# Weight passes in another order, and more seven-product pairs in the down projection, some with their weight sums made by DMA

## The chip, the cores and the metric

The kernel runs on one core of one Trainium2 chip. The metric is device time in microseconds of one execution; lower is better. Before the change the median of three runs is 1387.19 us (1386.93 to 1387.28).

## The reference

One layer of a hybrid decoder on 256 tokens of width 2048, all in float32:

```
h  = RMSNorm(x);  z = h @ W_in               # all projections of both kinds of heads, and two gates
A  = forgetting attention (8 heads of 128);  M = mLSTM (4 heads, 128 / 256)
merged = sigmoid(g_A) * (A @ P_A) + sigmoid(g_M) * (M @ P_M)
x  = x + merged @ W_out
u  = causal_dwconv3(RMSNorm(x) @ W_up)       # 2048 x 11264, each channel over three tokens
x  = x + (silu(u_gate) * u_val) @ W_down     # 5632 x 2048
```

The part at issue is the last two lines, the up product and the last product (the down projection), and in one detail the mLSTM's q and k projections.

## The kernel before, in words

**Products in parts.** TensorE multiplies float32 here in a one-pass form of rounded numbers. To keep accuracy each operand is split in a high and a low part: weights into `wh` (ScalarE, L170) and `wl = w - wh` (VectorE, L171), activations likewise (L198, L199). A product is then three passes: high by high, high by low, low by high.

**Weights.** They come in chunks of 1 MB ([128, 2048] float32), loaded on SP's queue into three buffers `raw` (L132). `split_sub` makes pieces of 1024 (or 512) columns of them, in four buffers each for `wh` and `wl`. `next_sub` hands a piece to TensorE, asks for the loads of the next two chunks, and has one to three further pieces split ahead. So a load waits until the third chunk before it has been split to its end.

**The up product** (`block_a`, `products_a`) has the weights as the stationary operand and 256 tokens as the moving one. For each 128 rows of the contraction there is a pass of 512 columns (`wh` by both parts of the activation, side by side) and one of 256 (`wl` by the high part). A block is 16 such pairs, 5632 rows of the output in 88 blocks by two halves `up` each; the convolution, gate and split of the result (`up_evac` and what follows) run on ScalarE and VectorE beside it. The mLSTM's q and k (`mq`, `mk`, 8 blocks) use the same function. `j` counts the 44 pairs of blocks (a gate and a value block); two `j` give a pair `m` of activation tiles, 22 pairs in all.

**The last product** (`s_block`, names `y0` and `y1` for the two halves of the output's columns) goes over these 22 pairs; here the activations are stationary and 512 weight columns move. A pair is a 2 by 2 block matrix (two tiles of tokens, two of the contraction, two of output columns). A plain pair ("p" in `Y_PAIRS`) takes eight products, 24 passes. A pair "S" uses Strassen's scheme in Winograd's form: seven products, 21 passes. For it sums of activations are made during up (`put_sums`, VectorE) and kept in DRAM (`s_dram`, written and read on POOL's queue; tiles `se` with a single buffer and `s_ops`), and sums of weights are made by VectorE just before their split: `b` (L155, 1024 columns), `b21` (L162, 512) and `t13` (L165, 512). A pair S has four pieces: the weights b11 and b22 as they are, b21, and the sums twice. Products of the four sub-blocks gather in PSUM (`y0q`, and `y0p` for those added to several results); after the last S some additions (`late`) bring them together.

**Order.** Every engine runs its instructions in order; a scheduler at build time sets the order on each engine from the program and its dependencies, and semaphores connect them. POOL's queue, in up, holds one write of `se` for each S, and in the last product the loads of `s_ops` and of the residual `xr`.

Of the kernel before, what the change touches and what calls it, by code (L numbers as in the profile page):

```python
# [10 lines left out]
F32 = mybir.dt.float32  # L11
# [6 lines left out]
P = 128  # L18
# [14 lines left out]

PLAIN = "p" * 8
G_PAIRS = "pSpSpSpp"
WO_PAIRS = "pSpSpSpp"
Y_PAIRS = "pp" + "SSp" * 2 + "Sp" + "SSp" * 3 + "Spp"
N_S = Y_PAIRS.count("S")  # L40

# [19 lines left out]
def trunk(ctx: ExitStack, tc: tile.TileContext, a):  # L61
# [28 lines left out]

    chunks, subs_of = [], []

    def add_chunk(ap, n, pieces=("whole", "whole")):

        subs_of.extend((len(chunks), i, kind) for i, kind in enumerate(pieces))
        chunks.append((ap, n, ap.tensor.name))

    def add_b(ap, n):
# [4 lines left out]
        add_chunk(a["w_mog0"][i], 2 * (MOG[0] + MOG[1]))  # L103
    add_b(a["w_mog1"], MOG[2])

    def add_pairs(ap, patterns):
        for i, kind in enumerate("".join(patterns)):
            pieces = ("b", "b21", "t13", "t24") if kind == "S" else ("whole", "whole")
            add_chunk(ap[i], 2048, pieces)

    for name in ("w_fox", "w_mqk", "w_mv"):
        add_b(a[name], 512)
# [21 lines left out]
    def split_sub(j):  # L134
        if j >= len(subs_of) or j in subs:
            return
        i, s, kind = subs_of[j]
# [3 lines left out]
        n = 512 if kind == "b21" else chunks[i][1] // 2  # L141
        raw, sums = raws[i], s_tiles.get("sums")


        if kind == "whole":
            src = raw[:, s * n : (s + 1) * n]
        elif kind == "b":
            src = raw[:, 512:1536]
            if s_tiles["of"] != chunks[i][2]:
                s_tiles["of"] = chunks[i][2]  # L150
                s_tiles["sums"] = a8(f"sums{i}", [2048])
            sums = s_tiles["sums"]

            with tc.issue_after(last_of["wl"].ins):
                nc.vector.tensor_tensor(  # L155
                    sums[:, :1024].rearrange("p (i c) -> p i c", i=2),
                    raw[:, :512].unsqueeze(1).to_broadcast([P, 2, 512]),
                    src.rearrange("p (i c) -> p i c", i=2), ALU.subtract,
                )
        elif kind == "b21":  # L160
            src = raw[:, 1536:]
            nc.vector.tensor_tensor(sums[:, 1024:1536], raw[:, 1024:1536], sums[:, :512], ALU.subtract)  # L162
        elif kind == "t13":
            src = sums[:, :1024]
            nc.vector.tensor_tensor(sums[:, 1536:], raw[:, 1536:], sums[:, 1024:1536], ALU.subtract)  # L165
# [4 lines left out]
        nc.scalar.activation(wh[:, :n], src, AF.Copy)  # L170
        last_of["wl"] = nc.vector.tensor_tensor(  # L171
            wl[:, :n], src, wh[:, :n].bitcast(F32), ALU.subtract
        )
        subs[j] = (wh[:, :n], wl[:, :n])
# [42 lines left out]
    def put_sums(src, dst, keep):  # L217

        a11, a21, a12, a22 = (src[:, i * P : (i + 1) * P] for i in range(4))
        n = 4 if keep else 3
        sv = scratch("sv", [P, n * P])
        s2, s3, s4 = (sv[:, i * P : (i + 1) * P] for i in range(3))
        s1 = sv[:, 3 * P :] if keep else a21
        nc.vector.tensor_tensor(s3, a21, a11, ALU.subtract)
        nc.vector.tensor_tensor(s1, a21, a22, ALU.add)
        nc.vector.tensor_tensor(s2, s1, a11, ALU.subtract)
        nc.vector.tensor_tensor(s4, a12, s2, ALU.subtract)
        put(dst[0], dst[1], sv)  # L230

    def mm(out, lhsT, rhs, start, stop):
# [47 lines left out]
    def s_block(name, pairs, s_ops, pattern, pools, dst, add=True, per_piece=0):  # L280


        q = [[pools[0](f"{name}q{tok}{h}") for h in range(2)] for tok in range(2)]
        ps, late, left = {}, [], pattern.count("S")
        n_s = left

        def prod(out, x, w, c, first, last):
            wh, wl = w[0][:, c * 512 : (c + 1) * 512], w[1][:, c * 512 : (c + 1) * 512]
            mm(out, x[1], wh, first, False)
            mm(out, x[0], wh, False, False)  # L290
            mm(out, x[0], wl, False, last)

        def piece():
            w = next_sub(4)
            for _ in range(min(2, len(late))):
                late.pop(0)()
            run_tasks(per_piece)
            return w

        def tt(o, x, y):  # L300
            late.append(lambda: nc.vector.tensor_tensor(o, x, y, ALU.add))

        for m, kind in enumerate(pattern):
            def op(i, tok):
                t = slice(tok * P, (tok + 1) * P)
                return pairs[m][:, i, 0, t], pairs[m][:, i, 1, t]

            if kind == "p":
                last = m == len(pattern) - 1
                ws = [piece(), piece()] if last else []  # L310

                todo = (
                    [(i, tok, h) for h in range(2) for tok in range(2) for i in range(2)] if last
                    else [(i, tok, h) for i in range(2) for h in range(2) for tok in range(2)]
                )
# [24 lines left out]
            if add:  # L340
                u3 = scratch("u3", [P, 512])
                late.append(lambda: nc.scalar.activation(u2, ps[1], AF.Copy))
                tt(c11, c11, ps[1])
                tt(u2, u2, ps[6])
                tt(u3, u2, ps[7])
                tt(u2, u2, ps[5])
                tt(c21, c21, u3)
                tt(u3, u3, ps[5])
                tt(c12, c12, u2)
                tt(c22, c22, u3)  # L350
            else:
                late.append(lambda: nc.scalar.activation(c11, ps[1], AF.Copy))
                tt(u2, c11, ps[6])
                tt(c21, u2, ps[7])
                tt(c12, u2, ps[5])
                tt(c22, c21, ps[5])
        for f in late:
            f()
        return q
# [36 lines left out]
    upper = const.tile([P, P], F32, name="upper")  # L396
    ones = const.tile([P, P], F32, name="ones")
    mhalf = const.tile([P, 8], F32, name="mhalf")
    mask_qk = const.tile([P, P], BF16, name="mask_qk")
    mask_st = const.tile([P, P], BF16, name="mask_st")  # L400

# [4 lines left out]

    def when_there(x):

        return nc.gpsimd.tensor_copy(mhalf[:, :1], x[:, :1].bitcast(F32))

    def make_constants():
        nc.gpsimd.memset(mhalf, -0.5)
# [517 lines left out]
    for j in range(NF):  # L930
# [19 lines left out]
        put_pair(g_pairs[m], gv)  # L950


    s_pos = [m for m, kind in enumerate(Y_PAIRS) if kind == "S"]
    ring = []

    def load_sums():
# [103 lines left out]
```

## Time and profile before

| | |
|---|---|
| median of three runs | 1387.19 us |
| the profiled execution, its own time | 1377.91 us |
| its span | 1376.1 us |
| granted TensorE clock | 1.000 |
| up product, about 667 to 1144 us | TensorE busy 477.0, VectorE 397.2, ScalarE 283.2 of 477.0 us |
| last product y0, 1144 to 1258 us | TensorE 113.7, VectorE 108.5, ScalarE 65.7 of 113.7 us |
| last product y1, 1258 to 1372 us | TensorE 113.7, VectorE 105.8, ScalarE 61.2 of 113.8 us |
| DMA over the span | 284 MB, mean 206 GB/s |

How to read it: a row of the page's groups names line, engine, operation, output and inputs, and the count. PE is TensorE's matmul, PEld its weight load. The chain that ended last is followed back from the last instruction; its pieces in order of time tell how long a run of passes of one kind took, with their count (`x48`). A window's row lists start and end, length, the busy time of each engine with its count of instructions, the granted clock, the DMA share and GB/s.

### The profile page before, as it was taken

To read this page: it belongs to the slowest core of one execution; us is meant where nothing else is said; L and a number is where in the kernel's file an instruction comes from. 1 tells how busy PE (TensorE), PEld (TensorE's weight loads), DVE (VectorE), ACT (ScalarE), POOL (GpSimd) and SP (SyncE) were. 2 spreads that over 40 slices of the span, in tenths; PEclk is the share of its full clock that TensorE was granted. 3 is DMA by queue.
4 is the path that set the end of the run, shared out by engine and by line. 5 is a ranking of instruction groups with operands and counts; after the bars stand their busy time and mean duration, and the time that the engine had idled before them with its cause. 6 is when DMAs were issued, how large, how long until landed. Compare 5 with 4: busy or idle time off the path is not lost.

```text
span 1376.1 us, 18451 instructions
## 1 busy us (share of the span) xinstructions
PE 1369.0 (99%) x6922; PEld 1158.1 (84%) x6922; DVE 1096.9 (80%) x1569; ACT 775.3 (56%) x1112; POOL 43.2 (3%) x77
## 2 busy tenths in 40 slices
PE   9999999999999999999999999999999999999998
PEld 8978888888888888888888888888888888878776
DVE  5655766556888867899888887888888888998998
ACT  6655554445665544465756565555555555564553
POOL 2101000000000000000000000000000000000000
PEclk9999999999999999999999999999999999999999
DMA  9644554443555556465555555555555566778853
GB/s 323 237 179 167 181 206 153 169 155 133 188 212 186 214 210 232 178 228 201 209 196 209 196 206 191 208 206 195 196 202 208 206 226 237 245 256 302 292 201 119
DMA packets 44649, 284.12 MB, mean 206 GB/s; under 512 B 5072, under 2 KB 5088, under 8 KB 13840
## 3 DMA queue, kind: packets, MB, share of 16 engines
q1 hardware_dynamic: 39168, 260.20, 52.6%
q0 software_dynamic: 5248, 22.74, 4.9%
q8 instruction: 54, 0.88, 0.3%
q14 instruction: 35, 0.29, 0.1%
q10 hardware_dynamic: 144, 0.02, 0.0%
HBM read 274.02 MB, written 8.91 MB: 206 GB/s over the span
## 4 chain that ended last, share of the span: by engine, by line
PE 99%; DVE 0%; DMA 0%; ACT 0%; issue 0%; ACTq 0%
PE up L233 35%; PE p L233 6%; PE y1q L233 6%; PE y0q L233 6%; PE mog L233 3%; PE fq L233 3%; PE g0q L233 3%; PE mv L233 3%; PE fk L233 3%; PE fv L233 3%; PE y0p L233 3%; PE y1p L233 3%; PE wo0q L233 2%; PE g1q L233 2%; PE g3q L233 2%; PE g2q L233 2%
## 5 line engine op out<-in xcount | busy, mean ns | idle before, releaser
L170 ACT ACTIVATE wh<-raw 128x1024 fp32r<-128x1024 f32 (+2 forms) x496 | 494.0, 1011 | 403.2 <-PE up L233 108.5
L171 DVE TENSOR_TENSOR wl<-raw,wh 128x1024 fp32r<-128x1024 f32 (+2 forms) x496 | 573.2, 1164 | 184.4 <-ACT wh L170 179.0
L233 PE MATMUL up<-h,wh 128*128 128x512 f32 x1408 | 488.8, 394 | 0.0
L233 PE MATMUL up<-h,wl 128*128 128x256 f32 x1408 | 390.2, 277 | 0.0
L233 PEld LDWEIGHTS up<-h,wh 128*128 128x128 f32 x1408 | 264.0, 188 | 61.4 <-DVE h L202 0.3
L233 PEld LDWEIGHTS up<-h,wl 128*128 128x128 f32 x1408 | 264.3, 188 | 0.2
L170 ACT ACTIVATE wh<-sums 128x1024 fp32r<-128x1024 f32 x78 | 82.8, 1062 | 118.4 <-PE y1q L233 24.6
L171 DVE TENSOR_TENSOR wl<-sums,wh 128x1024 fp32r<-128x1024 f32 x78 | 95.4, 1224 | 30.8 <-ACT wh L170 30.0
L918 DVE SCALAR_TENSOR_TENSOR t<-u,cst,t 128x256 f32<-128x256 f32 x176 | 84.9, 482 | 3.7 <-ACT t L916 0.7
L233 PE MATMUL p<-wh,am 128*128 128x512 f32 x256 | 79.6, 392 | 0.0
L233 PE MATMUL y1q<-wh,ghl 128*128 128x512 f32 x208 | 64.2, 390 | 0.0
L233 PE MATMUL y0q<-wh,ghl 128*128 128x512 f32 x208 | 64.2, 390 | 0.0
L233 PEld LDWEIGHTS p<-wh,am 128*128 128x128 f32 x256 | 47.6, 188 | 9.7
L916 ACT ACTIVATE t<-u,cst 128x256 f32<-128x256 f32 x88 | 52.0, 591 | 2.6 <-DVE u L913 2.2
L233 PE MATMUL p<-wl,am 128*128 128x512 f32 x128 | 49.9, 390 | 0.0
L155 DVE TENSOR_TENSOR sums<-raw 128x1024 f32<-128x1024 f32 x39 | 47.6, 1219 | 0.0
L233 PEld LDWEIGHTS y1q<-wh,ghl 128*128 128x128 f32 x208 | 39.1, 188 | 8.1
L233 PEld LDWEIGHTS y0q<-wh,ghl 128*128 128x128 f32 x208 | 39.0, 188 | 8.0
L233 PE MATMUL mog<-wh,hT 128*128 128x348 f32 (+1 forms) x192 | 42.5, 332 | 0.8 <-ACT wh L170 0.8
L233 PE MATMUL g0q<-wh,hN 128*128 128x512 f32 x128 | 41.2, 402 | 0.0
L233 PE MATMUL y1q<-wl,ghl 128*128 128x512 f32 x104 | 40.5, 390 | 0.0
L233 PE MATMUL y0q<-wl,ghl 128*128 128x512 f32 x104 | 40.5, 390 | 0.0
(370 smaller groups left out, 2110.0 us busy)
## 6 DMA issues: line engine op xcount, KB each, us to landing
raw<-in_w_up SPq DMA_DIRECT2D x88, 1024.0 KB, 4.8
raw<-in_w_dn SPq DMA_DIRECT2D x44, 1024.0 KB, 5.2
raw<-in_w_g SPq DMA_DIRECT2D x32, 1024.0 KB, 4.8
raw<-in_w_fox SPq DMA_DIRECT2D x24, 1024.0 KB, 4.9
raw<-in_w_p SPq DMA_DIRECT2D x16, 1024.0 KB, 4.9
raw<-in_w_out SPq DMA_DIRECT2D x16, 1024.0 KB, 4.9
s_ops<-s_dram POOLq DMA_DIRECT2D x12, 768.0 KB, 4.5
raw<-in_w_mqk SPq DMA_DIRECT2D x8, 1024.0 KB, 4.8
```

The lines of the kernel that those rows point to most:

```text
L155: nc.vector.tensor_tensor(sums[:, :1024].rearrange("p (i c) -> p i c", i=2), raw[:, :512].unsqueeze(1).to_broadcast([P, 2, 512]), src.rear ...
L170: nc.scalar.activation(wh[:, :n], src, AF.Copy)
L171: last_of["wl"] = nc.vector.tensor_tensor(wl[:, :n], src, wh[:, :n].bitcast(F32), ALU.subtract)
L233: last_of["mm"] = nc.tensor.matmul(out, lhsT, rhs, start=start, stop=stop)
L916: nc.scalar.activation(t, u[:, 2:], AF.Identity, scale=w[2], bias=w[3])
L918: nc.vector.scalar_tensor_tensor(out=t, in0=u[:, i : i + S], scalar=w[i], in1=t, op0=ALU.mult, op1=ALU.add)
```

## The change

1. `products_a` issues its passes in twos: two of 512 columns for two neighbouring contraction tiles, then the two of 256.
2. `Y_PAIRS` goes from `ppSSpSSpSpSSpSSpSSpSpp` to `pSZpSZSpSZpSZSpSZpSZpp`: 14 of 22 pairs with seven products instead of 12; eight are S, six are of a new kind Z.
3. For a Z the four blocks of weight sums lie ready in a DRAM tile `t`. They are made during the up product by six transfers on POOL's queue (three copies and three that add to what is there), one step for each `j`, each step behind a small copy that waits for `gv` of that `j`. Both halves have six, so there are 12 tiles and 72 transfers. In the last product a Z loads 1536 columns of its weights and 2048 of its `t`; its pieces need no sums on VectorE.
4. The signs of the sums are turned so that weights are only added (a DMA can add); activation sums and the last additions turn theirs to match. The waiting copy writes to a tile of its own, `seen`.

```diff
-Y_PAIRS = "pp" + "SSp" * 2 + "Sp" + "SSp" * 3 + "Spp"
-N_S = Y_PAIRS.count("S")
+Y_PAIRS = "p" + "SZpSZSp" * 2 + "SZpSZpp"
+N_S = len(Y_PAIRS) - Y_PAIRS.count("p")
...
     def add_pairs(ap, patterns):
         for i, kind in enumerate("".join(patterns)):
-            pieces = ("b", "b21", "t13", "t24") if kind == "S" else ("whole", "whole")
-            add_chunk(ap[i], 2048, pieces)
+            if kind == "Z":
+                t = dram.tile([P, 2048], F32, name=f"t{len(z_sums)}")
+                z_sums.append((t, ap[i]))
+                add_chunk(ap[i][:, 512:], 1536, (1024, 1536))
+                add_chunk(t, 2048)
+            else:
+                add_chunk(ap[i], 2048, ("b", "b21", "t13", "t24") if kind == "S" else None)
+
+    def sums_in_dram(i):
+
+        t, w = z_sums[i]
+        q = lambda x, n: x[:, n * 512 : (n + 1) * 512]
+        b12, b11, b22, b21 = (q(w, n) for n in range(4))
+        put_to = lambda o, x: lambda: nc.gpsimd.dma_start(o, x)
+        add_to = lambda o, x: lambda: nc.gpsimd.dma_start(o, x, accum_op=ALU.add)
+        return [
+            put_to(
+                t[:, :1024].rearrange("p (i c) -> p i c", i=2),
+                b12.unsqueeze(1).to_broadcast([P, 2, 512]),
+            ),
+            add_to(t[:, :1024], w[:, 512:1536]),
+            put_to(q(t, 2), q(t, 0)), add_to(q(t, 2), b22),
+            put_to(q(t, 3), q(t, 2)), add_to(q(t, 3), b21),
+        ]
...
     def products_a(z, act, ks, wh, wl, first, last):
 
-        for q, k in enumerate(ks):
-            ws = slice(q * P, (q + 1) * P)
-            mm(z, wh[:, ws], act[k].rearrange("p l s -> p (l s)"), first and q == 0, False)
-            mm(z[:, :S], wl[:, ws], act[k][:, 0, :], False, last and q == len(ks) - 1)
+
+        for q in range(0, len(ks), 2):
+            two = [(slice(i * P, (i + 1) * P), act[ks[i]]) for i in (q, q + 1)]
+            for i, (ws, x) in enumerate(two):
+                mm(z, wh[:, ws], x.rearrange("p l s -> p (l s)"), first and q + i == 0, False)
+            for i, (ws, x) in enumerate(two):
+                mm(z[:, :S], wl[:, ws], x[:, 0, :], False, last and q + i == len(ks) - 1)
...
         nc.vector.tensor_tensor(gv[:, (j % 2) * S : (j % 2 + 1) * S], sg, t, ALU.mult)
+
+        now = [(i, j - 1 - 3 * i) for i in range(len(z_sums)) if 0 <= j - 1 - 3 * i < 6]
+        if now:
+            with tc.issue_after(when_there(gv[:, (j % 2) * S :]).ins):
+                for i, step in now:
+                    sums_in_dram(i)[step]()
         if j % 2 == 0:
             continue
         m = j // 2
-        if Y_PAIRS[m] == "S":
+        if Y_PAIRS[m] != "p":
             se = big.tile([P, 2, 3 * P], F32R, tag="mv", name=f"se{m}")
```

How instructions stand on three engines, before and after (the numbers at names are those of buffers). TensorE inside a block of the up product, before:

```order
L233 MATMUL up_7263<-h_4800,wh_7266 128x512
L233 MATMUL up_7263<-h_4800,wl_7267 128x256
L233 MATMUL up_7263<-h_4800,wh_7266 128x512
L233 MATMUL up_7263<-h_4800,wl_7267 128x256
L233 MATMUL up_7263<-h_4800,wh_7266 128x512
L233 MATMUL up_7263<-h_4800,wl_7267 128x256
```

and after:

```order
L262 MATMUL up_7324<-h_4813,wh_7327 128x512 x2
L262 MATMUL up_7324<-h_4813,wl_7328 128x256 x2
L262 MATMUL up_7324<-h_4813,wh_7327 128x512 x2
L262 MATMUL up_7324<-h_4813,wl_7328 128x256 x2
L262 MATMUL up_7324<-h_4814,wh_7327 128x512 x2
```

The passes stand two and two; their number and shapes are the same. VectorE, the second seven-product pair of y0 and what follows it, before (an S: sums at L155, L162 and L165 between the low parts):

```order
L155 TENSOR_TENSOR sums_10405<-raw_10423 128x1024
L171 TENSOR_TENSOR wl_10479<-raw_10423,wh_10478 128x1024
L162 TENSOR_TENSOR sums_10405<-raw_10423,sums_10405 128x512
L171 TENSOR_TENSOR wl_10487<-raw_10423,wh_10486 128x512
L165 TENSOR_TENSOR sums_10405<-raw_10423,sums_10405 128x512
L171 TENSOR_TENSOR wl_10498<-sums_10405,wh_10497 128x1024
L171 TENSOR_TENSOR wl_10510<-sums_10405,wh_10509 128x1024
L171 TENSOR_TENSOR wl_10520<-raw_10461,wh_10519 128x1024
L171 TENSOR_TENSOR wl_10527<-raw_10461,wh_10526 128x1024
```

and after (a Z):

```order
L200 TENSOR_TENSOR wl_10586<-raw_10521,wh_10585 128x1024
L200 TENSOR_TENSOR wl_10593<-raw_10521,wh_10592 128x512
L200 TENSOR_TENSOR wl_10603<-raw_10569,wh_10602 128x1024
L200 TENSOR_TENSOR wl_10615<-raw_10569,wh_10614 128x1024
L200 TENSOR_TENSOR wl_10625<-raw_10612,wh_10624 128x1024
L200 TENSOR_TENSOR wl_10634<-raw_10612,wh_10633 128x1024
L184 TENSOR_TENSOR sums_10527<-raw_10631 128x1024
L200 TENSOR_TENSOR wl_10645<-raw_10631,wh_10644 128x1024
```

Of seven operations for the pair four are left, `raw_10569` being the chunk that holds the sums; the next S follows one plain pair later (L184). POOL's queue in the up product, before:

```order
L898 DMA xs<-x_4793 128x1024
L898 DMA xs<-x_4794 128x1024
L441 TENSOR_TENSOR r_127<-v,mhalf 128x2
L946 DMA s_dram<-se_6214 128x768
L946 DMA s_dram<-se_6436 128x768
```

and after:

```order
L444 COPY seen<-gv 128x1
L128 DMA t_75<-in_w_dn 128x2x512
L444 COPY seen<-gv 128x1
L129 DMA t_75<-in_w_dn 128x1024
L444 COPY seen<-gv 128x1
L128 DMA t_75<-t_75 128x512
L987 DMA s_dram<-se_6020 128x768
L444 COPY seen<-gv 128x1
L129 DMA t_75<-in_w_dn 128x512
L128 DMA t_76<-in_w_dn 128x2x512
L444 COPY seen<-gv 128x1
L128 DMA t_75<-t_75 128x512
```

Ahead of the first write of `se` there are now three steps of the first tile of sums, and between one such write and the next three or more transfers and their waiting copies; the second write of `se` stands two rows further down.

More of the change, by code (lines that the diff above doesn't have):

```diff
@@ L91, in trunk, with add_chunk @@
     chunks, subs_of = [], []
-    def add_chunk(ap, n, pieces=("whole", "whole")):
-        subs_of.extend((len(chunks), i, kind) for i, kind in enumerate(pieces))
+    def add_chunk(ap, n, pieces=None):
+        at = 0
+        for kind in pieces or (n // 2, n):
+            own = isinstance(kind, str)
+            subs_of.append((len(chunks), kind if own else "part", None if own else slice(at, kind)))
+            at = at if own else kind
         chunks.append((ap, n, ap.tensor.name))
@@ L104, in trunk @@
     add_b(a["w_mog1"], MOG[2])
+    z_sums = []
     def add_pairs(ap, patterns):
         for i, kind in enumerate("".join(patterns)):
-            pieces = ("b", "b21", "t13", "t24") if kind == "S" else ("whole", "whole")
-            add_chunk(ap[i], 2048, pieces)
+            if kind == "Z":
[20 more added lines that the diff above has]
+        ]
     for name in ("w_fox", "w_mqk", "w_mv"):
@@ L136, in split_sub @@
             return
-        i, s, kind = subs_of[j]
+        i, kind, cols = subs_of[j]
         load_chunk(i)
@@ L140, in split_sub @@
             put(hT[j][:, 0, :], hT[j][:, 1, :], xT[j], cst[:, C_G1 + j : C_G1 + j + 1])
-        n = 512 if kind == "b21" else chunks[i][1] // 2
+        n = 512 if kind == "b21" else cols.stop - cols.start if cols else chunks[i][1] // 2
         raw, sums = raws[i], s_tiles.get("sums")
-        if kind == "whole":
-            src = raw[:, s * n : (s + 1) * n]
+        if kind == "part":
+            src = raw[:, cols]
         elif kind == "b":
@@ L157, in split_sub @@
                     raw[:, :512].unsqueeze(1).to_broadcast([P, 2, 512]),
-                    src.rearrange("p (i c) -> p i c", i=2), ALU.subtract,
+                    src.rearrange("p (i c) -> p i c", i=2), ALU.add,
                 )
@@ L161, in split_sub @@
             src = raw[:, 1536:]
-            nc.vector.tensor_tensor(sums[:, 1024:1536], raw[:, 1024:1536], sums[:, :512], ALU.subtract)
+            nc.vector.tensor_tensor(sums[:, 1024:1536], raw[:, 1024:1536], sums[:, :512], ALU.add)
         elif kind == "t13":
             src = sums[:, :1024]
-            nc.vector.tensor_tensor(sums[:, 1536:], raw[:, 1536:], sums[:, 1024:1536], ALU.subtract)
+            nc.vector.tensor_tensor(sums[:, 1536:], raw[:, 1536:], sums[:, 1024:1536], ALU.add)
         else:
@@ L225, in put_sums @@
         s1 = sv[:, 3 * P :] if keep else a21
-        nc.vector.tensor_tensor(s3, a21, a11, ALU.subtract)
-        nc.vector.tensor_tensor(s1, a21, a22, ALU.add)
+        nc.vector.tensor_tensor(s3, a11, a21, ALU.subtract)
+        nc.vector.tensor_tensor(s1, a21, a22, ALU.subtract)
         nc.vector.tensor_tensor(s2, s1, a11, ALU.subtract)
-        nc.vector.tensor_tensor(s4, a12, s2, ALU.subtract)
+        nc.vector.tensor_tensor(s4, a12, s2, ALU.add)
         put(dst[0], dst[1], sv)
@@ L283, in s_block @@
         q = [[pools[0](f"{name}q{tok}{h}") for h in range(2)] for tok in range(2)]
-        ps, late, left = {}, [], pattern.count("S")
+        ps, late, left = {}, [], len(pattern) - pattern.count("p")
         n_s = left
@@ L298, in piece, with tt @@
             return w
-        def tt(o, x, y):
-            late.append(lambda: nc.vector.tensor_tensor(o, x, y, ALU.add))
+        def tt(o, x, y, op=ALU.add):
+            late.append(lambda: nc.vector.tensor_tensor(o, x, y, op))
         for m, kind in enumerate(pattern):
@@ L345, in s_block @@
                 tt(u3, u2, ps[7])
-                tt(u2, u2, ps[5])
+                tt(u2, ps[5], u2, ALU.subtract)
                 tt(c21, c21, u3)
-                tt(u3, u3, ps[5])
+                tt(u3, ps[5], u3, ALU.subtract)
                 tt(c12, c12, u2)
@@ L354, in s_block @@
                 tt(c21, u2, ps[7])
-                tt(c12, u2, ps[5])
-                tt(c22, c21, ps[5])
+                tt(c12, ps[5], u2, ALU.subtract)
+                tt(c22, ps[5], c21, ALU.subtract)
         for f in late:
@@ L398, in trunk @@
     mhalf = const.tile([P, 8], F32, name="mhalf")
+    seen = const.tile([P, 1], F32, name="seen")
     mask_qk = const.tile([P, P], BF16, name="mask_qk")
@@ L407, in when_there @@
     def when_there(x):
-        return nc.gpsimd.tensor_copy(mhalf[:, :1], x[:, :1].bitcast(F32))
+        return nc.gpsimd.tensor_copy(seen, x[:, :1].bitcast(F32))
     def make_constants():
@@ L950, in trunk @@
         put_pair(g_pairs[m], gv)
-    s_pos = [m for m, kind in enumerate(Y_PAIRS) if kind == "S"]
+    s_pos = [m for m, kind in enumerate(Y_PAIRS) if kind != "p"]
     ring = []
```

## The prediction, made before the change was run

> **What bounds the kernel now.** I read the page's busy shares and its chain first, then the stages as windows, then the chain in order of time, and last the waits of the last product.
>
> ```profile
> PE 1369.0 (99%) x6922; PEld 1158.1 (84%) x6922; DVE 1096.9 (80%) x1569; ACT 775.3 (56%) x1112; POOL 43.2 (3%) x77
> PE 99%; DVE 0%; DMA 0%; ACT 0%; issue 0%; ACTq 0%
> 667.13:1144.15 477.02, 477.02 (x2753) 417.04 (x2753) 397.20 (x645) 283.20 (x424) 7.70 (x14) 1.00 0.57 202
> 1144.15:1257.87 113.72, 113.72 (x493) 91.61 (x493) 108.51 (x121) 65.71 (x73) 3.70 (x7) 1.00 0.73 258
> 1257.87:1371.62 113.75, 113.74 (x492) 91.26 (x491) 105.83 (x115) 61.16 (x67) 2.85 (x5) 1.00 0.62 222
> ```
>
> The chain is TensorE from end to end. The three windows are the up product and the two halves of the last product (y0, y1): their length, busy time of PE, PEld, DVE, ACT and POOL, the granted clock (1.00 throughout), DMA share and GB/s. In y0 VectorE is busy 108.5 of 113.7 us, so it nearly sets the pace too. A busy PE is not a PE at its own pace, so I take the pace from chain rows without a wait.
>
> ```profile
> 47.39 7.61 PE mog L233 x48
> 667.13 477.02 PE up L233 x2752
> 1246.31 11.56 PE y0q L233 x51
> ```
>
> A pass of 512 columns takes 11.56/51 = 226.7 ns, a pass of 346 or 348 columns 7.61/48 = 158.5 ns. The slope is 68.2 ns over 165 columns, 0.413 ns each, which leaves about 15 ns per pass whatever its width. An up pair (512 and 256 columns) should then take 768 × 0.413 + 30 = 347 ns; the trace has 477.02/1376 = 346.7. So up runs on its passes alone, and only fewer or cheaper passes shorten it.
>
> In the last product that isn't so.
>
> ```profile
> 1157.09 2.04 PE y0p L233 x9
> 1161.85 2.45 PE y0p L233 x9
> 1172.48 2.04 PE y0p L233 x9
> 1177.24 2.44 PE y0p L233 x9
> PEld y1p L233 <- DVE wl L171: 3.5, 10, 0.4
> PEld y0p L233 <- DVE wl L171: 3.5, 10, 0.4
> ```
>
> Nine passes of a first seven-product pair take 2.04 us, 9 × 226.7 ns. In the second of two that follow each other the same nine take 2.45. The waits name the cause: the low weight parts from VectorE (L171), 20 waits, two in each of the ten places where the old pattern has "SS". Lost: 10 × 0.41 = 4.1 us.
>
> **The change part by part.** *Passes of the up product two and two.* Number and width of the passes stay (32 a block); only their order changes, in 88 up blocks and the 8 of the mLSTM q and k.
>
> ```profile
> 800.09 0.39 PE L233 MATMUL up<-h,wh 128*128 128x512 f32 x1
> 800.32 0.27 PE L233 MATMUL up<-h,wl 128*128 128x256 f32 x1
> 800.43 0.40 PE L233 MATMUL up<-h,wh 128*128 128x512 f32 x1
> 1162.14 0.39 PE L233 MATMUL y0p<-wh,s_ops 128*128 128x512 f32 x1
> 1162.50 0.50 PE L233 MATMUL y0p<-wl,ghl 128*128 128x512 f32 x1
> 1162.84 0.40 PE L233 MATMUL y0p<-wh,s_ops 128*128 128x512 f32 x1
> ```
>
> Each pass needs its own weights, loaded while the pass before runs. After a wait, where the next load has not run ahead, a 512 pass takes 0.34 us (1162.50 to 1162.84) instead of 0.227: an exposed load is worth 114 ns. Behind a short pass there are 0.11 to 0.12 us (800.32 to 800.43), so the load just fits. In the old order one of two loads stands behind a short pass, in the new one two of four: the same share. With a price per pass that does not depend on its neighbour, the new order is worth 0. That rests on the mog row alone. If instead time went with columns alone (226.7/512 = 0.443 ns), a pair would be 340 ns and 6.7 ns would be lost at the change of width; the new order has half as many such changes and would gain 3.4 ns × 1536 pairs (1408 + 128) = 5.1 us, at most 10.3. But mog passes would then take 153.6 ns, not 158.5. Upward, one extra fixed price in each group of four would be 15 ns × 768 = 11 us; the load that fits now speaks against it. I take 0.
>
> The Trainium skill (TensorE: Matmul & The Clock Gate, "Back-to-back issue gap") gives N/2.4 + 2.5 ns for a warm pass, some 325 ns a pair. The measured 346.7 is above that; by that rule, too, neighbours would not matter, and the sum stays.
>
> *Two more seven-product pairs.* 14 of 22 instead of 12: each saves one product of three passes in each half, 2 × 2 × 3 = 12 passes × 226.7 ns = 2.7 us. Their activation sums during up cost VectorE five more operations twice, under 2 us against its 477 − 397 = 80 us idle there: 0; without that cover it would be those 2 us.
>
> *Six pairs with sums from DRAM (Z).* Work of VectorE per pair, from starts of neighbours:
>
> ```profile
> 1164.80 1.22 DVE L171 TENSOR_TENSOR wl<-raw,wh 128x1024 fp32r<-128x1024 f32 x1
> 1165.93 1.22 DVE L155 TENSOR_TENSOR sums<-raw 128x1024 f32<-128x1024 f32 x1
> 1167.07 1.22 DVE L171 TENSOR_TENSOR wl<-raw,wh 128x1024 fp32r<-128x1024 f32 x1
> 1168.20 0.69 DVE L162 TENSOR_TENSOR sums<-raw,sums 128x512 f32<-128x512 f32 x1
> 1168.80 0.69 DVE L171 TENSOR_TENSOR wl<-raw,wh 128x512 fp32r<-128x512 f32 x1
> 1169.40 0.69 DVE L165 TENSOR_TENSOR sums<-raw,sums 128x512 f32<-128x512 f32 x1
> ```
>
> A 1024-wide one takes 1.14 us, a 512-wide one 0.60. S: 4 × 1.14 + 3 × 0.60 = 6.4 us against 21 passes, 4.8 us on PE. Z has no sums: 3 × 1.14 + 0.60 = 4.0 against 4.8. A plain pair: 2.3 against 5.4. So VectorE falls 1.6 us behind in an S, 3.2 in SS, and gains 0.8 in a Z. The old SS loses 0.41 at 3.2; an S alone loses nothing (2.04). The new runs are SZ (at most 1.6 behind) and four times SZS, 1.6 − 0.8 + 1.6 = 2.4 behind. Bounds for SZS: 0 and 0.41 each; being halfway between the two cases I take 0.2, 0.8 us in all. Stalls go from 4.1 to 0.8: −3.3 (−4.1 to −2.5).
>
> *Transfers.* A Z pair loads 1.75 MB instead of 1 MB, and each half loads one more tile of activation sums: 6 × 0.79 + 0.79 = 5.5 MB (10^6 bytes) per half. In y0 (258 × 113.7 + 5500)/110.8 = 314 GB/s, and the share goes from 0.73 to 0.89; in y1 to 0.78.
>
> ```profile
> GB/s 66 407 412 339 161 194 0 158 279 384 292 197 87 322 344 300 251 279 188 249 113 341 227 287 309 107 360 216 320 227 162 307 276 333 202 178 344 421 270 328
> raw<-in_w_up SPq DMA_DIRECT2D x88, 1024.0 KB, 4.8
> raw<-in_w_dn SPq DMA_DIRECT2D x44, 1024.0 KB, 5.2
> xs<-x POOLq DMA_DIRECT2D x4, 512.0 KB, 4.0
> xr<-xs POOLq DMA_DIRECT2D x2, 1024.0 KB, 8.5
> 852.55 16.87 SPq L132 DMA_DIRECT2D raw<-in_w_up  x4
> 864.01 1.06 ACT L170 ACTIVATE wh<-raw 128x1024 fp32r<-128x1024 f32 x1 [0.86 <-PE up L233]
> ```
>
> The first row is 1140 to 1260 us in 3 us slices: up to 421 GB/s are moved, so 314 fits, with queues in places. The likeliest place is the start of y1, where four output writes, the 1 MB of xr (8.5 us), two or three tiles of sums and the weights meet. I take 0.5 us, bounds 0 and 6 (0.5 us at each of 12 Z).
>
> In up POOL issues six transfers per Z, 72 in all, 0.5 MB twice and 0.25 MB four times, half of them adding. One step of a Z falls in each 11.1 us (64 passes), two Z overlapping. Plain copies 12.6 MB and adds 12.6 MB over some 420 us are 30 GB/s each; by 0.57 for 202 GB/s each is 0.085 of the engines. No row shows an adding transfer: at least it costs a plain one; I take 2 (two reads for one write). Share: 0.57 + 0.085 + 0.17 = 0.82. A load issued at 852.55 is read at 864.01: with 4.8 us to land it has 6.7 to spare, more than a 0.5 MB transfer (4.0 us) put ahead of it. A step has 11 us to land before the next needs it. So 0; without cover each delayed load would stop PE by what it is over 11.5 us.
>
> Signs that turn (subtract for add) keep every shape: 0. SP's queue gets 12 more loads, the first of them after the first sums stand in DRAM for some 400 us.
>
> Sum: 0 − 2.7 − 3.3 + 0.5 = −5.5 us. The profiled execution took 1377.9 us with a span of 1376.1, so it would be 1372.4; the median of the runs shown, 1387.2, is 9.3 above it, and I carry the difference over: **1381.7**.
>
> **The rivals.** *B, the order of the passes pays.* The 6.7 ns per pair hang on changes of width: −5.1 us more, 1376.6; at most 1371.4. For it: the width-proportional reading fits the 512 and 256 passes alone. Against it: mog.
>
> *C, loads become late in the last product.* Two chunks per Z pass through three buffers, PE needs 4.8 us for both, and a load takes 5.2.
>
> ```profile
> DMA  9644554443555556465555555555555566778853
> GB/s 323 237 179 167 181 206 153 169 155 133 188 212 186 214 210 232 178 228 201 209 196 209 196 206 191 208 206 195 196 202 208 206 226 237 245 256 302 292 201 119
> ```
>
> These are the page's 40 slices of 34.4 us: where y1 begins they show 302 and 292 GB/s at eight tenths, and 50 GB/s more is about 0.94. If each Z then stops PE by 0.3 to 0.6 us, 3.5 to 7 us go: 1385 to 1389. The Trainium skill (DMA: Bandwidth & Descriptors, "Where 436 GB/s comes from") puts the HBM side at about 358 GB/s for a core, by which that stretch would be full; the 421 in the row above speaks against it as a limit.
>
> *D, adds are slow; slower than before.* At a price of 4.1 plain transfers the up share is 1.0. Beyond it POOL, which waits in order for each step's predecessor, holds back the write of the activation sums behind it; their single buffer then holds VectorE at the next pair's sums, with the weight parts queued behind, and PE stops. At a price of 6 the share is 1.16: 0.16 × 420 = 67 us of transfers too much, of which the 22 us between pairs absorb a third: some 45 us, 1427. For it: no row bounds it. Against: four is far.
>
> *E, the second of two short passes waits a little for its load.* 15 ns in each of 768 groups, +11: 1393; above 7 ns the whole gain is gone.
>
> That the scheduler undoes the order is no rival: the rows of the order show two and two.
>
> **How the numbers follow.** Forecast 0.52 (its own range 1380 to 1385), B 0.12, C 0.21, D 0.09, E 0.06. About 0.2% (2.8 us) can be told from no change. Faster: forecast 0.50, B 0.12, the mild end of C 0.04: 0.66. Same: half of C 0.10, 0.04 from the others: 0.14. Slower: D, most of E and C's far end: 0.20. For 8 in 10 the range takes in the forecast, most of B and C: 1373 to 1391.
>
> **What would show it.** Up passes at 346.7 ns per pair: the order is worth nothing; 340 to 343 means B, more means E. In y a Z's nine passes at 2.04 us, SZS at 2.04 to 2.45, 972 passes: the other terms. PEld waiting for wl whose wh waited for raw means C. POOL's adds over 10 us, and up waiting on VectorE, mean D. Wrong above all would be a price of passes that depends on their neighbours.

## The result, and the profile after

The kernel after the change takes 1378.05 us (median of 6 runs, 1376.44 to 1380.82); beside it the kernel before took 1386.91 (6 runs, 1386.68 to 1387.28). The ratio is 0.9937, with a 95% interval of 0.9924 to 0.9950: 8.9 us less. Forecast were 1381.7, 5.5 less. One of the later runs of the kernel before (2444.89 us at a granted clock of 0.558) is a slow one and is left out of every count below.

The first thing to see is a contradiction. The two *profiled* executions hardly differ: 1377.91 us (span 1376.1) before, 1377.02 (span 1375.2) after. So the time that the timed runs gained is not to be found by laying these two profiles side by side, and that is what the experiments below are about.

The page's busy shares after, and the same three windows as in the prediction (length, busy PE, PEld, DVE, ACT, POOL, granted clock, DMA share, GB/s):

```profile
PE 1366.8 (99%) x6910; PEld 1156.9 (84%) x6910; DVE 1088.9 (79%) x1563; ACT 783.6 (57%) x1122; POOL 112.7 (8%) x192
667.13:1145.60 478.47, 478.47 (x2749) 417.50 (x2748) 398.59 (x653) 283.09 (x425) 76.30 (x127) 1.00 0.84 254
1145.60:1257.50 111.90, 111.75 (x489) 90.88 (x488) 102.91 (x111) 69.50 (x78) 4.25 (x8) 1.00 0.86 309
1257.50:1371.00 113.50, 111.96 (x486) 90.14 (x484) 101.54 (x109) 64.40 (x71) 3.36 (x6) 1.00 0.76 276
```

TensorE has 12 passes fewer (6910 for 6922), VectorE is busy 102.9 us in y0 where it was 108.5, and the DMA share in up is 0.84 where it was 0.57. Those are the changes as planned. Now the chain in order of time, start and length; first the kernel after, the second block of up and the long unbroken rest of it:

```profile
660.35 5.59 PE up L262 x32
666.37 479.30 PE up L262 x2752
```

479.30 us for 1376 pairs is 348.3 ns a pair. Against the row of before that the prediction is built on (477.02, 346.7 ns) up became 2.3 us *longer* in the profile. But that row has neighbours in the same chain of the profile before, which the prediction did not look at:

```profile
202.20 5.60 PE mq L233 x32
211.96 5.65 PE mq L233 x32
225.18 5.65 PE mk L233 x32
661.06 5.64 PE up L233 x32
```

Sixteen pairs in 5.60 to 5.65 us are 350 to 353 ns a pair, for passes of the same shapes in the same order. A slow first pass, about 80 ns longer than the others of its width, is part of each row. Behind it, by the starts of the passes, the block at 202 us runs at 346.6 ns a pair and the other three at 352.5 to 353.5. The long row begins at 667 behind two passes of another product (`ps_rb`, 0.43 us in the chain). So the pace of alternating passes was not one number in that profile either.

In the last product, first the chain of y0, two rows of a Z (nine passes in 2.04 us, that is without a wait) and the two places where a Z stands between two S:

```profile
1157.94 2.04 PE y0p L262 x9
1172.90 2.04 PE y0p L262 x9
1177.66 2.39 PE y0p L262 x9
1212.73 2.40 PE y0p L262 x9
```

and TensorE's weight loads' waits from 1140 to 1376 us (total, times, longest):

```profile
PEld y1p L262 <- DVE wl L200: 4.2, 7, 1.0
PEld y0p L262 <- DVE wl L200: 1.9, 5, 0.6
PEld y0q L262 <- DVE wl L200: 0.4, 2, 0.2
```

A Z alone costs nothing, as forecast; SZS loses 0.35 us, nearly as much as the old SS. The larger loss is new, and it is at the start of y1. There the chain leaves TensorE for a weight load:

```profile
1279.86 0.69 DVE sums L194
...
1280.62 6.53 DMA raw<-in_w_dn
...
1287.25 1.07 ACT wh L199
...
1291.38 1.15 DVE wl L200
...
1292.57 1.80 PE y1p L262 x6
```

A sum (L194) gives a buffer free at 1280.6, the load issued then takes 6.53 us to land, ScalarE and VectorE get their pieces late, and TensorE waits for the low part. ScalarE's waits for loads from 1270 to 1297 us (total, times, longest):

```profile
ACT wh L199 <- DMA raw<-in_w_dn: 8.8, 3, 5.7
```

The kernel before has no such wait from 1257 to 1300 us. What the DMA engines did from 1257 to 1300 us (1.1 us to a slice), after:

```profile
GB/s 297 396 269 276 343 227 133 261 396 343 248 156 354 440 432 421 415 402 423 402 438 432 412 417 436 442 412 267 351 328 229 335 392 398 410 431 406 427 415 299
DMA  8987858699968999999999999998996899999997
```

and before:

```profile
GB/s 351 293 341 345 238 263 402 320 191 259 396 396 396 236 297 404 229 91 198 404 339 177 412 417 413 429 434 419 427 259 0 154 394 427 450 297 91 335 412 137
```

From 1271 to 1286 us the kernel after moves 402 to 442 GB/s without a break; the kernel before reaches such rates too, but for 7.5 us at a stretch. By the starts of neighbouring passes TensorE loses 4.9 us in the last product: 3.0 between 1276 and 1294, three times 0.35 behind SZS, 0.5 at the end of y0 and small remainders. Before, counted in the same way, it lost 4.4.

The 3.0 belong to this one execution. The profiles of experiments 6 and 7 below, which have the same last product, lose 5.3 and 3.9 us at the start of y1. The timed runs of the kernel after spread over 4.4 us, those of the kernels without a Z in the last product (experiments 1, 3 and 4) over 1.8, 0.7 and 1.0; this fits loads that come late by a different amount each time, but is not shown to be that.

The transfers that up got are hidden. Size and median time to landing (page's DMA issues, kernel after):

```profile
raw<-in_w_up SPq DMA_DIRECT2D x88, 1024.0 KB, 6.8
t<-in_w_dn POOLq DMA_DIRECT2D x24, 512.0 KB, 9.4
t<-t POOLq DMA_DIRECT2D x24, 256.0 KB, 6.4
t<-in_w_dn POOLq DMA_DIRECT2D x24, 256.0 KB, 5.5
```

The weights of up land in 6.8 us instead of 4.8, at most in 10.1, with 11.5 allowed. The last row is adds alone: 256 KB added in 5.5 us, no longer than the plain copies of 256 KB in the row above it.

### The profile page after: what moved, and what is told of

It is laid out like the page before. It is cut to its first block, busy times and chain, and to the rows that moved or that the text cites. A ratio compares the mean times of both kernels' runs of the same rounds, so it can differ in the third digit from the quotient of the medians.

```text
span 1375.2 us, 18664 instructions
## 1 busy us (share of the span) xinstructions
PE 1366.8 (99%) x6910; PEld 1156.9 (84%) x6910; DVE 1088.9 (79%) x1563; ACT 783.6 (57%) x1122; POOL 112.7 (8%) x192
## 4 chain that ended last, share of the span: by engine, by line
PE 97%; DMA 1%; DVE 1%; ACT 0%; issue 0%; SPq 0%; ACTq 0%; DVEq 0%
PE up L262 36%; PE p L262 6%; PE y0q L262 5%; PE y1q L262 5%; PE fq L262 3%; PE g0q L262 3%; PE mv L262 3%; PE fk L262 3%; PE fv L262 3%; PE y0p L262 3%; PE mog L262 3%; PE wo0q L262 2%; PE g3q L262 2%; PE g2q L262 2%; PE g1q L262 2%; PE wo1q L262 2%
## 5 line engine op out<-in xcount | busy, mean ns | idle before, releaser
L199 ACT ACTIVATE wh<-raw 128x1024 fp32r<-128x1024 f32 (+3 forms) x520 | 518.3, 1010 | 426.1 <-PE up L262 111.1
L200 DVE TENSOR_TENSOR wl<-raw,wh 128x1024 fp32r<-128x1024 f32 (+3 forms) x520 | 598.4, 1161 | 188.9 <-ACT wh L199 180.9
L262 PE MATMUL up<-h,wh 128*128 128x512 f32 x1408 | 442.6, 396 | 0.0
L262 PE MATMUL up<-h,wl 128*128 128x256 f32 x1408 | 276.7, 278 | 0.0
L262 PEld LDWEIGHTS up<-h,wh 128*128 128x128 f32 x1408 | 214.6, 189 | 0.4 <-DVE h L231 0.2
L199 ACT ACTIVATE wh<-sums 128x1024 fp32r<-128x1024 f32 x62 | 65.8, 1061 | 87.6 <-DVE sums L194 13.0
L200 DVE TENSOR_TENSOR wl<-sums,wh 128x1024 fp32r<-128x1024 f32 x62 | 75.7, 1221 | 26.4 <-ACT wh L199 25.7
L184 DVE TENSOR_TENSOR sums<-raw 128x1024 f32<-128x1024 f32 x31 | 37.8, 1218 | 5.0 <-DMA raw<-in_w_dn 4.9
L444 POOL COPY seen<-gv 128x1 f32<-128x1 f32 x39 | 14.8, 380 | 321.4 <-DVE gv L974 321.4
L262 PE MATMUL mv<-wh,hT 128*128 128x512 f32 x128 | 40.2, 395 | 0.0
```

Source lines behind the costliest of these rows:

```text
L184: nc.vector.tensor_tensor(sums[:, :1024].rearrange("p (i c) -> p i c", i=2), raw[:, :512].unsqueeze(1).to_broadcast([P, 2, 512]), src.rear ...
L200: last_of["wl"] = nc.vector.tensor_tensor(wl[:, :n], src, wh[:, :n].bitcast(F32), ALU.subtract)
L262: last_of["mm"] = nc.tensor.matmul(out, lhsT, rhs, start=start, stop=stop)
L444: return nc.gpsimd.tensor_copy(seen, x[:, :1].bitcast(F32))
```

## The experiments

Two theories stand against each other at the start. By one, the order of the passes is worth nothing, as forecast, and the 8.9 us come from the last product. By the other the order carries most of it, in a way that the profile of before does not show.

### 1. Only the order

The kernel before with change 1 alone:

```diff
-        for q, k in enumerate(ks):
-            ws = slice(q * P, (q + 1) * P)
-            mm(z, wh[:, ws], act[k].rearrange("p l s -> p (l s)"), first and q == 0, False)
-            mm(z[:, :S], wl[:, ws], act[k][:, 0, :], False, last and q == len(ks) - 1)
+        for q in range(0, len(ks), 2):
+            two = [(slice(i * P, (i + 1) * P), act[ks[i]]) for i in (q, q + 1)]
+            for i, (ws, x) in enumerate(two):
+                mm(z, wh[:, ws], x.rearrange("p l s -> p (l s)"), first and q + i == 0, False)
+            for i, (ws, x) in enumerate(two):
+                mm(z[:, :S], wl[:, ws], x[:, 0, :], False, last and q + i == len(ks) - 1)
```

> The kernel before with one edit: the passes of products_a two and two. Theory 1 (the order is what the timed runs gained; the profiled execution of before, 1377.9 us against a median of 1386.9, did not pay what the alternating order costs in the other runs): about 1378 to 1380 us timed, 7 to 9 us under the kernel before, and a profiled span of 1376 to 1379 with up pairs at 347 to 348.2 ns. Theory 2 (the order is worth nothing; passes and stalls of the last product give the gain): 1386 to 1389 us timed.

Measured: 1379.88 us (1379.35 to 1381.11, 5 runs), ratio 0.9951 (0.9938 to 0.9963), 6.9 us under the 1386.81 of before. The chain has

```profile
667.88 479.30 PE up L233 x2752
```

to the hundredth of a us the length it has in the kernel after. So the order carries three quarters of the gain, although by the profile of before it should have cost 2.3 us.

### 2. Everything but the order

The kernel after, with the passes alternating again (the diff above backwards).

> The changed kernel with the alternating order of passes put back; 14 seven-product pairs and the sums from DRAM stay. Theory 1: the gain goes, 1384 to 1387 us timed, while the profiled execution stays near 1373 (up pairs 346.7 ns, 2.3 us less than with twos). Theory 2: as the changed kernel or up to 2 us faster, 1376 to 1378 timed.

Measured: 1386.20 us (1383.81 to 1388.09, 11 runs), ratio 0.9995 (0.9986 to 1.0003). The last product's part of the change, alone, cannot be told from nothing. The chain of its profile:

```profile
660.63 5.61 PE up L262 x32
666.67 483.36 PE up L262 x2736
...
1279.94 13.33 DMA raw<-t
```

Here up runs at 483.36/1368 = 353.3 ns a pair, with the same order of passes that took 346.7 in the profile of before and was expected to take 346.7 here. It cannot be the transfers, for experiments 3 and 4 have up with and without them. The last row is the crowd at the start of y1 again: a Z's sums take 13.33 us to land, and by the starts of the passes TensorE waits 2.1 us. It then pays a second time. Windows of the same profile (columns as above; the granted clock is the third number from the end):

```profile
1287.00:1288.50 1.50, 0.97 (x4) 0.66 (x4) 1.50 (x3) 0.91 (x1) 0.00 (x0) 1.00 1.05 421
1288.50:1290.00 1.50, 1.50 (x5) 1.19 (x5) 1.50 (x3) 0.38 (x1) 0.00 (x0) 0.59 1.05 430
1290.00:1292.00 2.00, 2.00 (x6) 1.44 (x5) 1.93 (x3) 2.00 (x3) 0.00 (x0) 0.50 1.05 397
1292.00:1294.00 2.00, 2.00 (x9) 1.61 (x9) 1.67 (x2) 0.77 (x2) 0.00 (x0) 0.95 0.98 392
```

and passes from its timeline (start, length):

```profile
1289.65 0.63 PE L262 MATMUL y1q<-wl,ghl 128*128 128x512 f32 x1
1290.07 1.05 PE L262 MATMUL y1p<-wh,ghl 128*128 128x512 f32 x2
1290.93 0.63 PE L262 MATMUL y1p<-wl,ghl 128*128 128x512 f32 x1
```

The granted clock falls to 0.50 for 3.4 us, and eight passes take 420 to 427 ns instead of 227: another 1.6 us. The Trainium skill (TensorE: Matmul & The Clock Gate, "Part 1: The HAM clock gate") states N/1.2 ns for a pass while the clock is gated, 426.7 ns at 512 columns, and a return to full rate after about 3.4 us of activity; this trace agrees in both. Of all the profiles here only this one has it; in the others the clock stays at 1.00 through the last product.

### 3. No Z: the same 14 pairs as S

```diff
-Y_PAIRS = "p" + "SZpSZSp" * 2 + "SZpSZpp"
+Y_PAIRS = "p" + "SSpSSSp" * 2 + "SSpSSpp"
```

There is then no tile `t`, and no transfer in up.

> The changed kernel with the six Z pairs as S: same 14 pairs, weight sums again on VectorE, no transfers for sums. VectorE is then 4.8 us behind after three S in a row (three times 1.6), so stalls in the last product grow from 4.9 us of the changed kernel to about 10 to 13: 5 to 8 us there. If the 1.4 ns that an up pair costs more in the changed kernel (348.1 against 346.7 ns) come from the transfers, 2 us of it come back in up; if they come from the order, they stay. So 1380 to 1385 timed.

### 4. The transfers, unused

The kernel after with all 72 transfers in up, but the six pairs treated as S in the last product, so that nothing reads the tiles:

```diff
                 z_sums.append((t, ap[i]))
-                add_chunk(ap[i][:, 512:], 1536, (1024, 1536))
-                add_chunk(t, 2048)
-            else:
-                add_chunk(ap[i], 2048, ("b", "b21", "t13", "t24") if kind == "S" else None)
+            add_chunk(ap[i], 2048, ("b", "b21", "t13", "t24") if kind != "p" else None)
```

> As the run without Z, but the 72 transfers that make the sums in DRAM still run in up; nothing reads them. The difference of the two is what the transfers cost in up. If they are hidden, as predicted: 0 within 1 us. If they cause the 1.4 ns per up pair: 2 us more than the run without Z, and up pairs at 348.1 ns here and 346.7 there.

Measured, together since they differ in the transfers alone: 1385.61 us without (1385.26 to 1385.94, 11 runs, ratio 0.9991, 0.9983 to 1.0000) and 1385.22 with them (1384.54 to 1385.55, 11 runs, ratio 0.9988, 0.9979 to 0.9997). The window of up without them:

```profile
667.50:1145.60 478.10, 478.10 (x2747) 417.13 (x2746) 398.19 (x652) 283.07 (x423) 8.77 (x16) 1.00 0.57 202
```

and with them:

```profile
667.50:1145.60 478.10, 478.10 (x2747) 417.16 (x2746) 398.22 (x653) 283.14 (x424) 76.27 (x127) 1.00 0.84 255
```

The chain without them, and then with them:

```profile
666.60 479.30 PE up L262 x2752
```
```profile
666.24 479.30 PE up L259 x2752
```

The DMA share goes from 0.57 to 0.84 and up stays at 479.30: 25 MB of copies and adds under the up product cost nothing. That also clears the transfers of the 1.6 ns a pair over 346.7; they belong to the order. What an S instead of a Z costs, the waits of experiment 3 show (1140 to 1380 us):

```profile
PEld y1p L262 <- ACT wh L199: 8.1, 11, 1.5
PEld y0p L262 <- ACT wh L199: 6.8, 10, 1.5
```

VectorE is too far behind in SS and SSS, and even the high parts come late. By the starts of the passes TensorE loses 12.8 us in the last product, within the 10 to 13 expected; the time, 1385.61, came out just above the 1380 to 1385 expected. Six Z in each half in place of six S are worth 1385.6 − 1378.05 = 7.6 us. But against the old pattern with 12 seven-product pairs, which had its S in pairs at most (experiment 1, 1379.88), the new one wins 1.8 us. The two were timed on separate occasions and their ranges overlap; the profiles agree, with 225.1 us from the first pass of the last product to its last, against 227.4 in experiment 1.

### 5. The kernel before, profiled once more

No edit. Experiment 2 had shown 353 ns a pair for the old order, the profile of before 346.7.

> The kernel before, unchanged, profiled once more. The earlier profile of it took 1377.9 us, its timed runs 1386.8; the changed kernel with the alternating order had up pairs at 353.9 ns in its profile. Theory 1 (the alternating order runs in one of two rhythms, and the earlier profile caught the quick one): up pairs at about 353 ns here and a time near 1386.8. Theory 2 (the kernel before always runs at 346.7 ns per pair, and the 9 us lie elsewhere): 346.7 ns again.

Measured: 1386.93 us, span 1385.1. The chain:

```profile
661.03 5.61 PE up L233 x32
667.07 483.01 PE up L233 x2734
```

483.01/1367 = 353.3 ns a pair, 6.6 more than in the first profile of the same program: times 1376 pairs 9.1 us, and the two spans differ by 9.0. Nothing else has moved. Distances between the starts of neighbouring passes in nanoseconds (512 columns, then 256, and so on), worked out from the records of these two profiles and of after, where up runs undisturbed:

```
before, first profile  233 117 231 113 | 232 118 231 112 | 233 117 231 113     346.7 a pair
before, profiled again 241 120 236 113 233 117 | 241 120 236 113 233 117       353.3 a pair
after (two and two)    233 231 113 119 | 233 236 116 113 | 233 231 113 119     348.3 a pair
```

The alternating order has two rhythms. One repeats after two pairs, one after three, and in the second the pass behind a short one takes up to 241 ns. Up to 661 us both profiles of before have the same rhythm in each block, now the one and now the other; they part only behind the two passes of `ps_rb` at 667. The timed runs of before say how often each is met there: three of 29 in this comparison lie between 1377.65 and 1378.18, the other 26 between 1386.35 and 1387.13; in an earlier one none of 27 is below 1386.36; in a later one four of 22 lie between 1377.72 and 1378.16, 17 between 1386.53 and 1387.34, and one, at 1380.03, in neither group. The distance of the two groups of 3 and 26, 9.0 us between their means, is that of the two profiles. So the profile that the prediction was given had caught the rarer rhythm, and 1387.2 is the time of the common one.

### 6. and 7. Eights and fours

If changes of width cost something, longer runs of one width should gain more than twos. The kernel after with

```diff
-        for q in range(0, len(ks), 2):
-            two = [(slice(i * P, (i + 1) * P), act[ks[i]]) for i in (q, q + 1)]
+        for q in range(0, len(ks), 8):
+            two = [(slice(i * P, (i + 1) * P), act[ks[i]]) for i in range(q, q + 8)]
```

and the same with 4.

> The changed kernel with the passes eight and eight: all eight of 512 columns of a piece, then its eight of 256. If time is lost where the width changes: an eighth of the changes of the alternating order, a quarter of twos; long passes then at 226.7 ns as in the last product, short at about 115: 342 ns per pair, 9 us less in up, 1369 to 1371 timed. If each pass has one fixed price (226.7 and 120 ns): 346.7, 2 us less than twos, 1376. If each short pass waits for the load behind it, whatever its neighbours: as twos, 348.3, 1378.

> The same, four and four. Loss at changes of width: half as many as twos, 345 ns per pair, about 1373 to 1374. Fixed price: 346.7, 1376. Load behind each short pass: 348.3, 1378.

Measured: eights 1379.47 us (1377.62 to 1380.82, 12 runs, ratio 0.9958, 0.9941 to 0.9975), fours 1381.56 (1380.31 to 1384.74, 12 runs, ratio 0.9979, 0.9960 to 0.9997). These ratios, and those of experiments 8 to 10, take in the quicker runs of before. Chain of eights:

```profile
666.78 480.45 PE up L262 x2752
```

and of fours:

```profile
666.76 482.73 PE up L262 x2752
```

That is 349.2 and 350.8 ns a pair, and none of the values expected. With a quarter and a half as many changes of width as twos both are longer. Time does not hang on the number of changes: rival B's reading falls. Nor are rival E's 15 ns there for a short pass behind a short one: in twos the two short passes take 113 and 119 or 116 and 113 ns, together about as much as two in the quick rhythm (113 and 117), and in eights the short ones take 113 to 120 ns each. Each order has a rhythm of its own. Of those run here, 348.3 of twos is the shortest that was the same in every profile of its order (six of them); eights and fours were profiled once.

### 8. Twos at the start of each half block, alternating behind it

Does the rhythm hang on the order alone, or on what came before it? Kernel of experiment 9 below, with

```diff
+        for q, k in enumerate(ks):
+            two = [(slice(i * P, (i + 1) * P), act[ks[i]]) for i in ((0, 1) if q == 0 else (q,))]
+            if q == 1:
+                continue
```

> The run with one Z of the second half as S, with passes alternating except the first two tiles of each half block, which stay two and two. The rhythm of the alternating order (346.7 or 353.3 ns per pair) holds through up where nothing interrupts it. If the order of passes sets it anew 176 times: every half block alike, all at 346.7 plus a little (1375 to 1377 timed) or all at 353.3 (1382 to 1384). If only a wait sets it, the rhythm found at the start of up stays in each execution, and times fall in two groups 8 to 9 us apart.

Measured: 1379.33 us (1377.54 to 1380.71, 12 runs, ratio 0.9964, 0.9945 to 0.9984). The chain, and, from the starts, the length of one half block of 16 passes after another (in nanoseconds; in the rhythms of before it is 2773 to 2774 or 2819 to 2831):

```profile
666.35 481.03 PE up L263 x2752
```
```
2777 2816 2777 2817 2776 2817 2777 2816 2777 2817 2776 2817
```

Neither rhythm holds: half blocks of one and the same order of passes take turns, one in the quicker rhythm (231 112 233 117 ...), the next in the slower (241 120 236 113 ...), 349.6 a pair on average. So a group of two long passes is enough to move the alternating order from one rhythm to the other, and the same passes take 2777 or 2817 ns depending on what ran before them. That is a price that depends on neighbours, and on more than the nearest.

### 9. y1's first Z as an S

Do the 3.0 us at the start of y1 (3.6 in the expectation) come from a Z's two loads, where four output writes, `xr`, activation sums and weights meet? The kernel after with y1 a pattern of its own (in y0 as it was):

```diff
+Y1_PAIRS = "pSSp" + "SZSp" + "SZpSZSp" + "SZpSZpp"
...
-    add_pairs(a["w_dn"], [Y_PAIRS] * 2)
+    add_pairs(a["w_dn"], [Y_PAIRS, Y1_PAIRS])
```

> The changed kernel with the first of the six Z pairs of the second half as S (0.75 MB less to load where that half begins). If the 3.6 us that TensorE lost there in the changed kernel's profile (1277 to 1294 us) come from late loads: they fall below 1 us, less 0.4 for one run SS more, so 2 to 3 us faster, 1375 to 1376 timed. If they come from VectorE: as the changed kernel or slower, 1378 to 1379.

Measured: 1376.76 us (1375.62 to 1377.91, 12 runs), against 1386.90 of before beside it; the ratio is 0.9940 (0.9923 to 0.9956). TensorE's waits at the start of y1, 1270 to 1300 us:

```profile
PEld y1p L263 <- DVE wl L201: 2.4, 4, 1.0
PE y1p L263 <- DVE wl L201: 0.9, 2, 0.5
```

and in the kernel after, 1270 to 1297 us:

```profile
PEld y1p L262 <- DVE wl L200: 3.5, 5, 1.0
PE y1p L262 <- DVE wl L200: 1.4, 3, 0.6
```

By the starts of the passes 1.8 us are lost there instead of 3.0, not less than 1 as expected. So the loads of one Z have a part in the loss, and the rest has another cause or other loads. The median is the lowest of all versions run, 1.3 us under the kernel after, though that was timed on another occasion and the ranges overlap.

### 10. The residual's load later

Experiment 9 with `xr` of y1 (1 MB on POOL's queue) loaded behind four more tiles of activation sums instead of at the start of y1:

```diff
+        if b == 1 and m == s_pos[8]:
+            with tc.issue_after(last_of["sums"].ins):
+                load_xr()
...
-        nc.gpsimd.dma_start(xr, xs[:, :, c0 : c0 + 1024])
+        if b == 0:
+            load_xr()
```

> The run with one Z of the second half as S, with the load of the residual xr moved later in POOL's queue there, behind four loads of activation sums that it held up. If the 2 us that TensorE still lost near 1287 us in that run come from loads that crowd there: they shrink to about 1, 1375.5 to 1376 timed against 1376.8. If the loads just move together and crowd elsewhere: 1376.5 to 1378.

Measured: 1377.10 us (1375.53 to 1381.17, 12 runs, ratio 0.9945, 0.9926 to 0.9964): no gain over experiment 9. In the profile TensorE loses 3.7 us from 1260 to 1300 us, against 2.3 there. Its waits from 1260 to 1300 us still have

```profile
ACT wh L200 <- DMA raw<-in_w_dn: 3.4, 1, 3.4
DVE sums L185 <- DMA raw<-in_w_dn: 2.0, 1, 2.0
```

Loads stay late without `xr` there, so it was not `xr` alone that made the crowd. What else could be moved was not tried.

## Why the prediction was right, and where it was not

The direction, the range and roughly the time came out; the split did not. The sum put 0 on the order and −5.5 on the last product. The runs put −6.9 on the order (experiment 1) and about −1.8 on the last product (kernel after against experiment 1, with ranges that overlap; with the old order −0.6, experiment 2, whose interval reaches from −1.9 to +0.4). That the time came out within 4 us of the forecast is luck: only a third of the gain that was forecast is there, and a gain that was put at nothing made up the rest.

*The order, 0.* This step failed, at "with a price per pass that does not depend on its neighbour". It was checked on one long row, 346.7 ns a pair, that agreed with prices taken from `mog`. The row was true, but of one rhythm; the same program mostly runs up at 353.3, and twos run it at 348.3 in every profile. Per pair 353.3 − 348.3 = 5.0 ns, times 1376 pairs 6.9 us: that is experiment 1's gain, whole. The last sentence of the prediction named what would make it wrong, and the rows at 202 to 661 us of the profile before already showed it.

*The Trainium skill's rule for the gap between passes.* The prediction took from the Trainium skill (TensorE: Matmul & The Clock Gate, "Back-to-back issue gap") that neighbours would not matter. The Trainium skill gives N/2.4 + 2.5 there for an isolated pass only, and says in the same section that in a stream of weight loads and passes both set the spacing; so the prediction read more out of the formula than stands there. The measurement decides: 346.7, 348.3, 349.2, 350.8 and 353.3 ns for the same pair of passes in different order or after a different past.

*9.3 us carried over.* The prediction saw that the profiled execution stood 9.3 us under the median, and carried the difference over as though it lay around the kernel. It was the clue: 9 us are inside up. Carried over, it made the sum come out near the truth for a wrong reason: against the profile's 346.7 the order *costs* 2.3 us, and the gain is that the 9 us of the slower rhythm no longer come up.

*12 passes fewer, −2.7.* Right: 6910 for 6922, at 2.04 us for nine in the rows above.

*Stalls, −3.3.* The mechanism was right, the size not. SZ costs nothing and SZS something; but each SZS loses 0.35, not 0.2, the upper bound of 0.41 nearly, and there is 0.5 at the end of y0. SZS puts VectorE 2.4 us behind by the working, and that already costs nearly what SS cost at 3.2. Outside the start of y1 the stalls went from 4.4 (4.1 in the prediction, which counted the ten SS alone) to some 1.9: −2.5.

*Late loads in the last product, +0.5.* Mis-sized: 3.0 us. This is rival C, at the place it named, at about half its price. The mean of 309 GB/s in y0 (314 forecast) was right and of no use; the late loads stand in the 15 us where all queues together move 402 to 442 GB/s. That the crowd makes them late is argued from the place, and experiment 9 bears it out in part.

*The Trainium skill's figure for the HBM side.* The Trainium skill (DMA: Bandwidth & Descriptors, "Where 436 GB/s comes from") puts that limit at about 358 GB/s for a core, which is a stack's 716 divided by two cores. One core runs here, and these 15 us at 402 to 442 show that 358 is not its limit.

The three terms of the last product are −2.7 − 2.5 + 3.0 = −2.2 by the two profiles, near the −1.8 between the kernels.

*Transfers in up, 0.* Right, and shown by experiments 3 against 4. The share was forecast at 0.82 and is 0.84, with adds priced at two copies each.

*The rivals.* B's side is where the gain lay, but its mechanism, a price for each change of width, falls with fours and eights. D falls: adds land as fast as copies. E falls by the starts of the short passes in twos and eights. C happened in part.

What stays open is what makes the alternating order take one rhythm or the other. The traces show that it can change at an interruption by passes of another product (in the mLSTM's q and k, and at 667 us) and then holds, for 480 us in up; experiment 8 shows that two long passes in a row can switch it. That it is the moment of the restart against some clock of the chip is a guess, and was not tested.

## What to carry to other kernels

Before building on a profile, hold its own time against the median of the timed runs: if they differ by more than the runs do among themselves, the profile shows another execution than the one that is paid for, and the difference has a place in the trace. Read a repeated pattern's pace in several places, behind several interruptions; where it is not the same, the order of passes is worth a try, because an order whose pace is always the same can beat one that is quicker on a lucky day. And when work is handed from an engine to DMA, look for the few microseconds where all queues have work at once; the mean share of a stage does not show a load that comes late.

## What the runs showed of the hardware

- Passes of 512 and 256 columns, each with weights of its own, cost 346.7 to 353.3 ns a pair with the same work, by order and past. Two and two, the length repeats to the hundredth: 479.30 us for 2752 passes in six different kernels (after, experiments 1, 3, 4, 9 and 10).
- The alternating order can run undisturbed for 480 us in either of two rhythms, and one program has both, 9 us apart in its time. Shorter blocks of the same order, 16 to 48 passes, show both within one execution.
- Waits of TensorE of 2.1 us in all, within 3.0 us, cost 1.6 us more through a half clock for 3.4 us (experiment 2). In experiment 6 waits of 2.6 us in all, within 3.5 us, left it at 1.00.
- Transfers that add in DRAM (256 KB) took 5.5 us to landing, copies of that size 6.4 (medians of 24 each, in the kernel after); the core moved 402 to 442 GB/s for 15 us.
